# Last layer norm of a hybrid encoder layer: one broadcast product in place of two scalings, shared by two engines

## The chip, the core and the metric

The kernel runs on one core of one Trainium2 chip. Its engines are TensorE (PE in the profile; PEld is its weight load), VectorE (DVE), ScalarE (ACT), GpSimd (POOL) and the queue on which it starts nearly all transfers (SP). Each engine works through its own list of instructions in order and waits where a semaphore tells it to. The metric is device time in microseconds (us), the median of several runs.

## The reference, cut to what matters

One layer over 1024 prompt and 32 sample positions (1056 columns when stored transposed), model width 1024, hidden width 4096, all in float32. The change lies in the last third:

```python
x = _layernorm(ALPHA * x + mix, ln1_g, ln1_b)
hid = jax.nn.relu(x @ w_ff1)
ff = (hid * hid) @ w_ff2
x = _layernorm(ALPHA * x + ff, ln2_g, ln2_b)
# _layernorm: (x - mean) * rsqrt(var + eps) * g + b, over the 1024 features
```

## The kernel before, in words

Features lie on the partitions (8 blocks of 128), positions on the free axis. Every float32 matmul is done as three: each operand is split into a high part in a shorter format and the rest (`split`, L104 to L111: ACT copies the high part in L108, DVE or POOL subtracts it in L111), and `three` (L856 to L860) issues high by high, high by low and low by high.

The second matrix product of the MLP is mostly done by a seven-product scheme (Strassen-Winograd) over halves of the features and of the 1056 columns. Its two blocks of sums, `z`, are four tiles of two feature blocks each. The hidden blocks outside that scheme (`CLASSIC`, four of them) are multiplied plainly, in quarters of 264 columns.

The program from there on is a list of steps. Each step has loads, preparations (`prep`: splits of weights and activations), matmuls and a `post` part. `run` (L1146) writes the loads of a step six steps ahead of its matmuls and its preparations three steps ahead, so this list sets the order on all engines; nothing is reordered afterwards. At the very beginning `run` holds the preparations back to two until the first steps are written.

The end of the list, in order of the matmuls:

- `P4`: four steps of 24 matmuls, the last product that runs over all four feature blocks at once. Its post adds what was kept in buffers (`fold`, L1018, eight on DVE and four on POOL) and then the accumulators (`add_z`, L1011).
- `qs[0]`, `qs[1]` (q0 and q1 below): eight steps each, one for each feature block, of 12 matmuls with the plain weights `ew`. Each ends with an add of the accumulator into `z` on DVE (L1259).
- `M5`: four steps of 24 matmuls (add in L1125). `M3[0]`: four steps of 12 matmuls (add in L1130; M30 below). Each step of M3 needs all four pairs of blocks, that is four weights and four activations, which its preparation `prep3` makes in three groups: pair 0, pair 1, and pairs 2 and 3 together. For each pair DVE first forms the weight by a subtraction (`add_w`, L853), ACT and POOL split it, and ACT and DVE split the activation.
- `qs[2]` (q2), `M3[1]` (M31), `qs[3]` (q3): 8, 4 and 8 steps of 12 matmuls.

An accumulator is one of four slots of PSUM in rotation.

As soon as a quarter of 264 columns is complete in `z`, its layer norm is worked off between the steps that follow. `ln2_parts` (L1218) gives the parts: three totals on POOL (L1225); `centre`, in which PE sums over the partitions (`small_sum`, L1205 to L1208, two matmuls by a matrix of 1/1024), DVE subtracts the mean from the four tiles (L1233), ACT squares (L1235, L1238) and POOL adds the squares (L1239); `root`, another sum on PE, a square root on ACT (L1244) and a reciprocal on DVE (L1245); and `scaled_out` twice, which for each feature block multiplies by gain and reciprocal root on DVE (L1214), adds the bias on ACT (L1215) and starts the store (L1216). A table at the end of the function says behind which step each part stands.

The last quarter, q3, has a form of its own, `last_quarter` (L1262). Behind q3's third step it sums two blocks on PE for an offset (`offset`; L1289 on ACT), which DVE subtracts from blocks 0 to 3 and POOL from blocks 4 to 7 (L1276); it adds blocks and squares as they come (`square`: ACT L1281, DVE L1283 and L1284); and when the last block is there, `end` sums on PE, subtracts the remaining mean (L1311, tiles 0 and 1 on DVE, 2 and 3 on POOL), takes the root (ACT L1314, DVE L1316) and calls `scaled_out` for all eight blocks. q2's last parts stand between q3's steps.

Of the kernel before, what the change touches and what calls it, by code (L numbers as in the profile page):

```python
# [69 lines left out]
def hybrid_layer(ctx, tc, xT, win, wkw, wo, w1, w2, ckT, cv, ckiT, scT, cw, lnp, rb, cst, oh,  # L70
# [621 lines left out]
    st = {}  # L692
# [328 lines left out]
    def ff2_chunk(ci, pairs):  # L1021
# [45 lines left out]

        def by_features(form, xn, place, post, groups):

            got = {p: {} for p in pairs}  # L1070

            def load(p):
                def f():
                    got[p]["raw"] = hidden_raw()
                    nc.sync.dma_start(got[p]["raw"], hd[p, FORM[xn]])
                return f

            def prep(*ps):
                def f():
                    raw = [form(p) for p in ps]  # L1080
                    for p, r in zip(ps, raw):
                        w, x = place(pairs.index(p))
                        split(got[p]["raw"], *x, lo_eng=V)
                        split(r, *w)
                        got[p]["w"], got[p]["x"] = w, x
                return f

            def step(d, cs):
                acc = []

                def mm():
                    acc.append(new_acc())
# [7 lines left out]
            return [load(p) for p in pairs], [prep(*ps) for ps in groups], step  # L1100

# [36 lines left out]
        if ends:  # L1138
            P5 = by_features(lambda p: n1[p], "t1", place5, post5, [(p,) for p in pairs])
            P3 = by_features(lambda p: add_w(A["12", p], n2[p], OP.subtract), "22", place3, post3, [pairs[:1], pairs[1:2], pairs[2:]])  # L1140
            return P1, P2, P6, P7, P4, P5, P3
# [4 lines left out]
    def run(steps, ahead, ahead_load):  # L1146

        n, prepared = len(steps), 0
        for i in range(-ahead_load, n):
            if i + ahead_load < n:  # L1150
                for f in steps[i + ahead_load].load:
                    f()
            while prepared < min(n, i + ahead + 1 if i > 0 else min(2, i + ahead + 1)):
                for f in steps[prepared].prep:
                    f()
                prepared += 1
            if i >= 0:
                for f in steps[i].mm + steps[i].post:
                    f()
# [50 lines left out]

    def scaled_out(c0, n, rstd, js):
        for j in js:
            zj = z[j // 2][:, j % 2, c0:c0 + n]
            V.scalar_tensor_tensor(zj, zj, lnw[:, 2, j:j + 1], rstd, op0=OP.mult, op1=OP.mult)  # L1214
            S.activation(zj, zj, AF.Identity, bias=lnw[:, 3, j:j + 1])  # L1215
            nc.sync.dma_start(yT[j * 128:j * 128 + 128, c0:c0 + n], zj)  # L1216

    def ln2_parts(c0, n):  # L1218
        cols = slice(c0, c0 + n)
# [21 lines left out]
        def root():  # L1241
# [4 lines left out]

        return (total(1), total(2), total(3), centre, root, lambda: scaled_out(c0, n, got["rstd"], range(4)),
                lambda: scaled_out(c0, n, got["rstd"], range(4, 8)))

# [15 lines left out]
    def last_quarter():  # L1265
# [26 lines left out]

        def begin():
            got["sums"] = unit("s1")
            for i in range(4):
                centre(i, V)
                square(i)

        def end():
# [8 lines left out]
            for i in range(4):  # L1308
# [37 lines left out]
    for d in range(3):  # L1346
        P4[1 + d].post.insert(0, fold(d, 0, 1, V))
    (load5, prep5, step5), (load3, prep3, step3) = P5, P3
    M5 = [step5(d, (0, 1)) for d in range(4)]
    M3 = [[step3(d, (c,)) for d in range(4)] for c in range(2)]  # L1350
    steps += qs[0] + qs[1] + M5 + M3[0] + qs[2] + M3[1] + qs[3]
    for j in range(4):
        for m, st in enumerate((qs[0][j // 2], qs[0][4 + j // 2])):
            load, prep = classic_w(j, m)
            st.load.append(load)
            st.prep.append(prep)
        qs[0][5 + j // 2].load.append(load5[j])
        qs[1][3 + j].prep.append(prep5[j])
        M5[1 + j // 2].load.append(load3[j])
    for f, st in zip(prep3, (M5[3], M3[0][0], M3[0][1])):  # L1360
        st.prep.append(f)
    for q, when in ((0, (qs[1][2], qs[1][7], M5[0], M5[1])),
                    (1, (M5[1], M3[0][3], qs[2][2], qs[2][5])),
                    (2, (M3[1][1], qs[3][1], qs[3][2], qs[3][3]))):
        when = (qs[q][3], qs[q][5], qs[q][7]) + when
        for f, st in zip(ln2_parts(q * Q, Q), when):
            st.post.append(f)
# [85 lines left out]
```

## Time and profile before

| what | value |
|---|---|
| device time, median of 3 runs | 1344.34 us (1343.89 to 1350.7) |
| the profiled execution, its own time | 1348.35 us |
| its span (first to last recorded work) | 1346.6 us |
| PE busy | 1245.1 us, 92% of the span |
| DVE busy | 994.9 us, 74% |
| ACT busy | 692.8 us, 51% |
| POOL busy | 564.6 us, 42% |
| granted TensorE clock, mean | 0.967 |

All rows below are of the profiled execution; times are microseconds from the start of its span. The shares are averages over stages with different limits, so what a change in one stage is worth has to be read from that stage's rows.

### The profile page before, as it was taken

Reading aid. Unit: us, or ns where it says so; the run is one execution under the profiler, and the core shown is the slowest. Engines: PE = TensorE matmul, PEld = TensorE weight load, DVE = VectorE, ACT = ScalarE, POOL = GpSimd, SP = SyncE. Lnnn points to the kernel's source line nnn. Section 1 sums busy time; section 2 is a strip of 40 time slices with the busy share of each in tenths; the row PEclk is TensorE's granted clock in tenths of the full one; section 3 lists DMA queues with packets and bytes.
Section 4 is the critical chain, followed back from the end, with each engine's and each line's share of the span. In section 5 each row is a group of like instructions: output and inputs, shape, how many; then the busy total and the mean of one; then the engine's idle time right before and its main releaser. Section 6 shows DMA issues by size and latency. Waiting matters only on the chain. (4 is left out here: it accounts for less than half of the span.)

```text
span 1346.6 us, 24097 instructions
## 1 busy us (share of the span) xinstructions
PE 1245.1 (92%) x8822; PEld 1203.5 (89%) x8822; DVE 994.9 (74%) x2043; ACT 692.8 (51%) x1378; POOL 564.6 (42%) x452
## 2 busy tenths in 40 slices
PE   7999999897899988896899999999999999998984
PEld 6999999897788987785899999999999999998884
DVE  5675899999488889878657667666557668586766
ACT  6666988644688878784322222222343444443323
POOL 2412344513521252363453553454445444447632
PEclk9999999899899998988899999999999999998987
DMA  6221111134531221243134343443863663542201
GB/s 209 92 68 37 48 33 47 48 108 152 166 87 18 47 65 32 71 141 122 45 108 150 138 153 139 147 154 137 302 234 91 196 187 113 176 144 87 65 33 65
DMA packets 97222, 149.98 MB, mean 111 GB/s; under 512 B 12456, under 2 KB 41808, under 8 KB 97104
## 3 DMA queue, kind: packets, MB, share of 16 engines
q1 hardware_dynamic: 81664, 139.55, 31.7%
q0 software_dynamic: 9504, 4.33, 1.9%
q10 hardware_dynamic: 5936, 4.58, 1.2%
q8 instruction: 69, 1.13, 0.4%
q14 instruction: 49, 0.40, 0.1%
HBM read 105.41 MB, written 43.00 MB: 110 GB/s over the span
## 5 line engine op out<-in xcount | busy, mean ns | idle before, releaser
L111 POOL TENSOR_TENSOR whl<-wraw,whl 128x512 fp32r<-128x512 f32 (+1 forms) x184 | 251.0, 1369 | 429.6 <-ACT whl L108 408.8
L858 PE MATMUL acc<-b,whl 128*128 128x264 f32 x1088 | 310.9, 286 | 6.1 <-DVE ring L937 3.0
L859 PE MATMUL acc<-b,whl 128*128 128x264 f32 x1088 | 310.7, 286 | 0.0
L860 PE MATMUL acc<-b,whl 128*128 128x264 f32 x1088 | 309.4, 284 | 0.0
L858 PEld LDWEIGHTS acc<-b,whl 128*128 128x128 f32 x1088 | 205.6, 189 | 7.1 <-DVE ring L937 3.2
L860 PEld LDWEIGHTS acc<-b,whl 128*128 128x128 f32 x1088 | 206.1, 189 | 0.0
L859 PEld LDWEIGHTS acc<-b,whl 128*128 128x128 f32 x1088 | 205.1, 189 | 0.1
L108 ACT ACTIVATE whl<-wraw 128x512 fp32r<-128x512 f32 (+1 forms) x184 | 113.1, 623 | 175.3 <-DVE wraw L853 143.2
L131 PE MATMUL mm<-xh,whl 128*128 128x384 f32 (+4 forms) x520 | 172.3, 332 | 14.3 <-ACT whl L108 5.6
L132 PE MATMUL mm<-area,whl 128*128 128x384 f32 (+4 forms) x552 | 182.9, 332 | 0.4 <-DVE area L111 0.4
L133 PE MATMUL mm<-xh,whl 128*128 128x384 f32 (+4 forms) x520 | 169.6, 331 | 0.0
L111 DVE TENSOR_TENSOR b<-xraw,b 128x528 fp32r<-128x528 f32 x94 | 69.7, 742 | 87.1 <-ACT b L108 87.0
L108 ACT ACTIVATE b<-xraw 128x528 fp32r<-128x528 f32 x94 | 60.5, 644 | 136.0 <-PE acc L860 82.1
L441 ACT ACTIVATE junka<-s,cand 128x1024 bf16<-128x1024 f32 (+1 forms) x93 | 96.5, 1037 | 42.0 <-DVE cand L454 34.2
L131 PEld LDWEIGHTS mm<-xh,whl 128*128 128x128 f32 (+1 forms) x520 | 97.9, 188 | 18.1 <-issue 8.1
L132 PEld LDWEIGHTS mm<-area,whl 128*128 128x128 f32 (+1 forms) x552 | 104.5, 189 | 2.9 <-DVE area L111 0.8
L133 PEld LDWEIGHTS mm<-xh,whl 128*128 128x128 f32 (+1 forms) x520 | 97.6, 188 | 3.2 <-POOL whl L111 1.2
L111 POOL TENSOR_TENSOR whl<-at,whl 128x512 fp32r<-128x512 f32 x56 | 81.5, 1465 | 30.8 <-ACT whl L108 30.8
L443 DVE TENSOR_SCALAR_CACHE_REDUCE junk<-s,cand 128x384 bf16<-128x384 f32 (+1 forms) x124 | 80.2, 647 | 1.3
L858 PE MATMUL acc<-area,whl 128*128 128x264 f32 x240 | 69.0, 288 | 0.0
L859 PE MATMUL acc<-area,whl 128*128 128x264 f32 x240 | 68.7, 286 | 0.0
L860 PE MATMUL acc<-area,whl 128*128 128x264 f32 x240 | 68.5, 286 | 0.0
(310 smaller groups left out, 3345.9 us busy)
## 6 DMA issues: line engine op xcount, KB each, us to landing
hd<-ring SPq DMA_DIRECT2D x98, 264.0 KB, 2.1
xraw<-hd SPq DMA_DIRECT2D x98, 264.0 KB, 2.7
at<-in_w_dram SPq DMA_DIRECT2D x58, 256.0 KB, 3.7
wraw<-in_win_dram SPq DMA_DIRECT2D x52, 256.0 KB, 2.6
wraw<-in_wo_dram SPq DMA_DIRECT2D x40, 256.0 KB, 2.7
w_a<-in_w_dram SPq DMA_DIRECT2D x23, 256.0 KB, 3.7
w_c<-in_w_dram SPq DMA_DIRECT2D x19, 256.0 KB, 3.4
zz<-zd SPq DMA_DIRECT2D x4, 1056.0 KB, 8.4
```

The costliest lines, as they stand in the source:

```text
L108: S.activation(hi, raw, AF.Copy)
L111: (lo_eng or G).tensor_tensor(lo, raw, f32(hi), op=OP.subtract)
L131: PE.matmul(ps, wh[k], a, start=(k == 0), stop=False)
L132: PE.matmul(ps, wh[k], b, start=False, stop=False)
L133: PE.matmul(ps, wl[k], a, start=False, stop=(k == K - 1))
L441: S.activation(junk(R, N), s, AF.Sign, bias=c, scale=-1.0, accum_out=cnt[:R, i:i + 1])
L443: V.tensor_scalar(junk(R, N), s, c, -float(k), op0=OP.is_ge, op1=OP.add, accum_out=cnt[:R, i:i + 1])
L858: PE.matmul(ps, wh, xhi, start=start, stop=False, skip_group_check=more)
L859: PE.matmul(ps, wh, xlo, start=False, stop=False, skip_group_check=more)
L860: PE.matmul(ps, wl, xhi, start=False, stop=stop, skip_group_check=more)
```

## The change

It does several things to the end of the program and one to its middle.

- `scaled_out` is taken apart. `scaled` multiplies a tile (two feature blocks, 128x528) by the reciprocal root, broadcast over the two blocks, on an engine that is given to it; `out` applies gain and bias in one ACT operation for each block and starts the store. Quarters 0 and 2 are scaled on POOL, quarter 1 on DVE, the last on DVE (tiles 0, 1, 2) and POOL (tile 3).
- The parts of the layer norms stand behind other, mostly later steps. Quarter 1's `centre` moves from M5's second step to M30's second, its `root` from M30's fourth step to q2's sixth. `offset` stands one step earlier (behind q3's second step), the offset's subtraction is divided over two steps, and q2's `root` and its scaling and outputs stand two to four steps later in q3.
- Three of the four weights for `prep3` are formed behind q0's fifth to seventh steps (`make`). The low parts of the activations of pairs 1 and 3 are subtracted on POOL instead of DVE.
- The plain weights `ew` are loaded and split for one step at a time, from P4 on, where they were split two at a time from q0 on.
- `run` no longer holds back the first preparations.

```diff
@@ by_features
+            def make(p):
+                def f():
+                    got[p]["form"] = form(p)
+                return f
...
-                    raw = [form(p) for p in ps]
-                    for p, r in zip(ps, raw):
+                    for p in ps:
+                        if "form" not in got[p]:
+                            make(p)()
+                    for p in ps:
                         w, x = place(pairs.index(p))
-                        split(got[p]["raw"], *x, lo_eng=V)
-                        split(r, *w)
+                        split(got[p]["raw"], *x, lo_eng=lo_eng(pairs.index(p)))
+                        split(got[p]["form"], *w)
@@ run
-            while prepared < min(n, i + ahead + 1 if i > 0 else min(2, i + ahead + 1)):
+            while prepared < min(n, i + ahead + 1):
@@ the layer norm
-    def scaled_out(c0, n, rstd, js):
-        for j in js:
+    def scaled(c0, n, rstd, parts, eng):
+        for i in parts:
+            zi = z[i][:, :, c0:c0 + n]
+            eng.tensor_tensor(zi, zi, rstd[:, None].to_broadcast([128, 2, n]), op=OP.mult)
+
+    def out(c0, n, parts):
+        for j in [2 * i + a for i in parts for a in range(2)]:
             zj = z[j // 2][:, j % 2, c0:c0 + n]
-            V.scalar_tensor_tensor(zj, zj, lnw[:, 2, j:j + 1], rstd, op0=OP.mult, op1=OP.mult)
-            S.activation(zj, zj, AF.Identity, bias=lnw[:, 3, j:j + 1])
+            S.activation(zj, zj, AF.Identity, scale=lnw[:, 2, j:j + 1], bias=lnw[:, 3, j:j + 1])
             nc.sync.dma_start(yT[j * 128:j * 128 + 128, c0:c0 + n], zj)
@@ last_quarter, end
-                if i > 0:
-                    scaled_out(c0, n, rstd, range(2 * i - 2, 2 * i if i < 3 else 8))
+            for i, e in ((0, V), (3, G), (1, V), (2, V)):
+                scaled(c0, n, rstd, (i,), e)
+                out(c0, n, (i,))
...
-        steps[2].post.append(offset)
-        steps[3].post.append(begin)
+        steps[1].post.append(offset)
+        steps[2].post.append(lambda: begin(0, 1))
+        steps[3].post.append(lambda: begin(2, 3))
@@ where the parts stand
+        if j < 3:
+            qs[0][4 + j].post.append(make3[j])
-        for m, st in enumerate((qs[0][j // 2], qs[0][4 + j // 2])):
+        for m, st in enumerate((P4[j], qs[0][j])):
...
-                    (1, (M5[1], M3[0][3], qs[2][2], qs[2][5])),
+                         (1, V, (M3[0][1], qs[2][5], M3[1][0], M3[1][2], M3[1][1], M3[1][2], M3[1][3], qs[3][0])),
```

DVE's list from q0's root to M30, before (`wraw` is a formed weight, `area` an activation for M30, `zz` the four tiles of z, `at` the reciprocal root):

```order
L1245 RECIPROCAL at<-at 128x264
L853 TENSOR_TENSOR wraw_6871<-w_b,at 128x512
L111 TENSOR_TENSOR area<-xraw_6872,area 128x528
...
L1214 SCALAR_TENSOR_TENSOR zz_10814<-zz_10814,lnw,at 128x264 x2
L1214 SCALAR_TENSOR_TENSOR zz_10846<-zz_10846,lnw,at 128x264 x2
L1233 TENSOR_TENSOR zz_10514<-zz_10514,acc 128x2x264
...
L853 TENSOR_TENSOR wraw_6871<-w_b,at 128x512 x2
L111 TENSOR_TENSOR area<-xraw_6872,area 128x528 x2
```

The same stretch of DVE's list now (L1257 is the reciprocal, L1132 the add of M5, L1245 the subtraction of `centre`):

```order
L1257 RECIPROCAL at<-at 128x264
L111 TENSOR_TENSOR area<-xraw_6872,area 128x528
L1132 TENSOR_TENSOR zz_10814<-acc,zz_10814 128x528
...
L853 TENSOR_TENSOR wraw_6871<-w_b,at 128x512
L111 TENSOR_TENSOR area<-xraw_6872,area 128x528
...
L1137 TENSOR_TENSOR zz_10514<-acc,zz_10514 128x264 x2
L1245 TENSOR_TENSOR zz_10514<-zz_10514,acc 128x2x264
```

One formed weight and two activations are left in the stretch; the eight scalings of quarter 0 are gone from it and quarter 1's subtraction stands behind M30's first two adds.

POOL's list at the end of the program, before (L1239 adds squares, L1276 subtracts the offset, L1311 the mean):

```order
L1239 TENSOR_TENSOR w_d<-w_d 128x528
L1276 TENSOR_TENSOR zz_10814<-zz_10814,at 128x264 x2
L1276 TENSOR_TENSOR zz_10846<-zz_10846,at 128x264 x2
L1311 TENSOR_TENSOR zz_10814<-zz_10814,at 128x2x264
L1311 TENSOR_TENSOR zz_10846<-zz_10846,at 128x2x264
```

POOL's list there now (L1288 is the offset, L1222 the broadcast product, L1324 the mean):

```order
L1288 TENSOR_TENSOR zz_10846<-zz_10846,at 128x264 x2
L1222 TENSOR_TENSOR zz_10514<-zz_10514,at 128x2x264
L1222 TENSOR_TENSOR zz_10547<-zz_10547,at 128x2x264
L1222 TENSOR_TENSOR zz_10814<-zz_10814,at 128x2x264
L1222 TENSOR_TENSOR zz_10846<-zz_10846,at 128x2x264
L1324 TENSOR_TENSOR zz_10814<-zz_10814,at 128x2x264
L1324 TENSOR_TENSOR zz_10846<-zz_10846,at 128x2x264
L1222 TENSOR_TENSOR zz_10846<-zz_10846,at 128x2x264
```

Quarter 2's four products have come between the offset and the last mean, and one product of the last quarter stands at the end.

ACT's last rows now (L1293 squares, L1317 to L1327 belong to `end`, L1227 is `out`):

```order
L1227 ACTIVATE zz_10514<-zz_10514,lnw 128x264 x2
L1293 ACTIVATE at<-zz_10846 128x264
L1227 ACTIVATE zz_10547<-zz_10547,lnw 128x264 x2
L1227 ACTIVATE zz_10814<-zz_10814,lnw 128x264 x2
L1293 ACTIVATE w_d<-zz_10846 128x264
...
L1327 ACTIVATE at<-w_d,eps 128x264
L1227 ACTIVATE zz_10514<-zz_10514,lnw 128x264 x2
L1227 ACTIVATE zz_10846<-zz_10846,lnw 128x264 x2
L1227 ACTIVATE zz_10547<-zz_10547,lnw 128x264 x2
L1227 ACTIVATE zz_10814<-zz_10814,lnw 128x264 x2
L1227 ACTIVATE zz_10846<-zz_10846,lnw 128x264 x2
```

Six outputs of quarter 2 stand among the last two squares, and its last two stand behind the eight of quarter 3, where ten outputs now end the list instead of eight.

## Rows read from the trace of the kernel before

**Rows 1.** PE's waits from 600 us on: total us, times, longest us

```profile
PE acc L1208 <- DVE w_d L1283: 6.1, 1, 6.1
...
PE acc L858 <- DVE zz L1011: 5.9, 3, 4.5
PE acc L858 <- ACT w L108: 5.1, 1, 5.1
...
PE acc L858 <- ACT ring L908: 1.6, 2, 0.9
```

**Rows 2.** Busy us (instructions) of PE, PEld, DVE, ACT, POOL; PEclk, DMA share, GB/s

```profile
1240.00:1250.00 10.00, 10.00 (x84) 10.00 (x83) 3.54 (x8) 0.00 (x0) 3.12 (x4) 1.00 0.00 0
1280.00:1290.00 10.00, 7.16 (x27) 6.19 (x28) 7.21 (x9) 1.68 (x3) 5.04 (x4) 0.54 0.00 0
```

**Rows 3.** PE's timeline in M30: start, us, line, out<-in [idle before <-releaser]

```profile
1281.28 0.59 PE L858 MATMUL acc<-area,w 128*128 128x264 f32 x1 [5.10 <-ACT w L108]
```

**Rows 4.** The chain that ended last, PE's sum behind M30: start, us

```profile
1292.57 0.89 PE acc L1208 x4
```

**Rows 5.** DVE's timeline from M5 to M30

```profile
1270.27 0.68 DVE L853 TENSOR_TENSOR wraw<-w_b,at 128x512 f32<-128x512 f32 x1
...
1273.33 1.70 DVE L1214 SCALAR_TENSOR_TENSOR zz<-zz,lnw,at 128x264 f32<-128x264 f32 x4
1274.94 2.54 DVE L1233 TENSOR_TENSOR zz<-zz,acc 128x528 f32<-128x528 f32 x4
1277.40 3.16 DVE L853 TENSOR_TENSOR wraw<-w_b,at 128x512 f32<-128x512 f32 x2
1280.49 3.50 DVE L111 TENSOR_TENSOR area<-xraw,area 128x528 fp32r<-128x528 f32 x2
```

**Rows 6.** ACT's timeline at M5's start and before M30's weights

```profile
1262.89 0.48 ACT L1244 ACTIVATE at<-acc,eps 128x264 f32<-128x264 f32 x1 [3.28 <-PE acc L1208]
...
1280.60 0.63 ACT L108 ACTIVATE w<-wraw 128x512 fp32r<-128x512 f32 x1 [1.08 <-DVE wraw L853]
```

**Rows 7.** POOL's timeline, weight splits for M30

```profile
1266.90 1.76 POOL L111 TENSOR_TENSOR whl<-wraw,whl 128x512 fp32r<-128x512 f32 x1
1272.04 1.29 POOL L111 TENSOR_TENSOR whl<-wraw,whl 128x512 fp32r<-128x512 f32 x1 [3.38 <-ACT whl L108]
...
1281.69 3.43 POOL L111 TENSOR_TENSOR w<-wraw,w 128x512 fp32r<-128x512 f32 x2
```

**Rows 8.** DVE's timeline beside a busy POOL, folds and quarter 0's centring

```profile
1223.55 10.41 DVE L1018 TENSOR_TENSOR zz<-zz,w_b 128x528 f32<-128x528 f32 x6
...
1254.41 2.55 DVE L1233 TENSOR_TENSOR zz<-zz,acc 128x528 f32<-128x528 f32 x4 [0.50 <-PE acc L1208]
```

**Rows 9.** POOL's timeline in the same two stretches

```profile
1223.02 3.50 POOL L111 TENSOR_TENSOR ew<-w_d,ew 128x512 fp32r<-128x512 f32 x2
...
1251.25 4.71 POOL L111 TENSOR_TENSOR whl<-w_d,whl 128x512 fp32r<-128x512 f32 x3
```

**Rows 10.** DVE's timeline in the last quarter and at the end

```profile
1319.02 3.20 DVE L1214 SCALAR_TENSOR_TENSOR zz<-zz,lnw,at 128x264 f32<-128x264 f32 x4
...
1332.85 0.42 DVE L1259 TENSOR_TENSOR zz<-acc,zz 128x264 f32<-128x264 f32 x1
...
1337.00 1.80 DVE L1316 RECIPROCAL at<-at 128x264 f32<-128x264 f32 x1
1338.84 3.32 DVE L1214 SCALAR_TENSOR_TENSOR zz<-zz,lnw,at 128x264 f32<-128x264 f32 x8
```

**Rows 11.** POOL's timeline in the last quarter and at the end

```profile
1319.31 3.53 POOL L1276 TENSOR_TENSOR zz<-zz,at 128x264 f32<-128x264 f32 x4 [4.06 <-ACT at L1289]
1335.36 2.56 POOL L1311 TENSOR_TENSOR zz<-zz,at 128x528 f32<-128x528 f32 x2 [12.52 <-ACT at L1307]
```

**Rows 12.** ACT's timeline: last square, and the last eight outputs

```profile
1333.36 0.42 ACT L1281 ACTIVATE w_d<-zz 128x264 f32<-128x264 f32 x1 [0.90 <-DVE zz L1259]
...
1339.36 3.35 ACT L1215 ACTIVATE zz<-zz,lnw 128x264 f32<-128x264 f32 x8 [2.40 <-DVE zz L1214]
```

More of the change, by code (lines that the diff above doesn't have):

```diff
@@ L1066, in product, with by_features @@
             return out
-        def by_features(form, xn, place, post, groups):
+        def by_features(form, xn, place, post, groups, lo_eng):
             got = {p: {} for p in pairs}
@@ L1099, in step @@
                 return Step(mm=[mm], post=[lambda: post(d, acc[0], cs)])
-            return [load(p) for p in pairs], [prep(*ps) for ps in groups], step
+            return [load(p) for p in pairs], [make(p) for p in pairs], [prep(*ps) for ps in groups], step
         def new_pair():
@@ L1138, in ff2_chunk @@
         if ends:
-            P5 = by_features(lambda p: n1[p], "t1", place5, post5, [(p,) for p in pairs])
-            P3 = by_features(lambda p: add_w(A["12", p], n2[p], OP.subtract), "22", place3, post3, [pairs[:1], pairs[1:2], pairs[2:]])
+            P5 = by_features(lambda p: n1[p], "t1", place5, post5, [(p,) for p in pairs], lambda i: V)
+            P3 = by_features(lambda p: add_w(A["12", p], n2[p], OP.subtract), "22", place3, post3, [pairs[:1], pairs[1:2], pairs[2:]],
+                             lambda i: G if i % 2 else V)
             return P1, P2, P6, P7, P4, P5, P3
@@ L1209, in small_sum, with ln2_parts @@
         return ps
-    def scaled_out(c0, n, rstd, js):
-        for j in js:
+    def scaled(c0, n, rstd, parts, eng):
[4 more added lines that the diff above has]
+        for j in [2 * i + a for i in parts for a in range(2)]:
             zj = z[j // 2][:, j % 2, c0:c0 + n]
-            V.scalar_tensor_tensor(zj, zj, lnw[:, 2, j:j + 1], rstd, op0=OP.mult, op1=OP.mult)
-            S.activation(zj, zj, AF.Identity, bias=lnw[:, 3, j:j + 1])
+            S.activation(zj, zj, AF.Identity, scale=lnw[:, 2, j:j + 1], bias=lnw[:, 3, j:j + 1])
             nc.sync.dma_start(yT[j * 128:j * 128 + 128, c0:c0 + n], zj)
-    def ln2_parts(c0, n):
+    def ln2_parts(c0, n, eng):
         cols = slice(c0, c0 + n)
@@ L1245, in root @@
             V.reciprocal(got["rstd"], got["rstd"])
-        return (total(1), total(2), total(3), centre, root, lambda: scaled_out(c0, n, got["rstd"], range(4)),
-                lambda: scaled_out(c0, n, got["rstd"], range(4, 8)))
+        return [total(1), total(2), total(3), centre, root, lambda: scaled(c0, n, got["rstd"], range(2), eng),
+                lambda: scaled(c0, n, got["rstd"], range(2, 4), eng)] + [lambda i=i: out(c0, n, (i,)) for i in range(4)]
     def plain_step(q, d):
@@ L1291, in offset, with begin @@
                 centre(i, G)
-        def begin():
-            got["sums"] = unit("s1")
-            for i in range(4):
+        def begin(*ds):
+            if ds[0] == 0:
+                got["sums"] = unit("s1")
+            for i in ds:
                 centre(i, V)
@@ L1347, in hybrid_layer @@
         P4[1 + d].post.insert(0, fold(d, 0, 1, V))
-    (load5, prep5, step5), (load3, prep3, step3) = P5, P3
+    (load5, _, prep5, step5), (load3, make3, prep3, step3) = P5, P3
     M5 = [step5(d, (0, 1)) for d in range(4)]
@@ L1361, in hybrid_layer @@
         st.prep.append(f)
-    for q, when in ((0, (qs[1][2], qs[1][7], M5[0], M5[1])),
-                    (1, (M5[1], M3[0][3], qs[2][2], qs[2][5])),
-                    (2, (M3[1][1], qs[3][1], qs[3][2], qs[3][3]))):
+    for q, eng, when in ((0, G, (qs[1][2], qs[1][7], M5[3], M3[0][0], M3[0][0], M3[0][1], M3[0][2], M3[0][3])),
+                         (1, V, (M3[0][1], qs[2][5], M3[1][0], M3[1][2], M3[1][1], M3[1][2], M3[1][3], qs[3][0])),
+                         (2, G, (M3[1][1], qs[3][3], qs[3][4], qs[3][5], qs[3][5], qs[3][6], qs[3][6], qs[3][7]))):
         when = (qs[q][3], qs[q][5], qs[q][7]) + when
-        for f, st in zip(ln2_parts(q * Q, Q), when):
+        for f, st in zip(ln2_parts(q * Q, Q, eng), when):
             st.post.append(f)
```

## The prediction

> **What bounds the kernel now.** I first read the list of PE's waits. From 600 us on three waits of 4.5 to 6.1 us stand out in the part that the change touches [rows 1]: the first plain step of q0 waits for an accumulator that DVE's adds (L1011) free, M30 waits for a weight of pair 2 that ACT splits, and the closing sum of q3 waits for DVE's sums. Then the table by stretches: beside an undisturbed stretch with 84 matmuls in 10 us, that is 0.119 us each, the stretch with M30's wait has 27, at a granted clock of 0.54, near the lower of its two levels (1.2 of 2.4 GHz) [rows 2]. So a wait of PE costs itself and a slow time behind it. The timelines then show who made M30 wait. The wait ends at 1281.28 and is 5.10 long [rows 3]. ACT could split the weight at 1280.60, when DVE had formed it [rows 6]. DVE formed it late (two forms in 3.16 from 1277.40) because four scalings of quarter 0 and the four subtractions of quarter 1's centre stood ahead of it (1.70 and 2.54), and then took 3.50 for two activations while POOL split weights [rows 5, 7]. The chain puts M30's end at 1292.57 [rows 4].
>
> Before the end DVE is the bound. PE waits 6.1 for the closing sum, and DVE's last add ends at 1332.85 + 0.42 = 1333.27 [rows 1, 10], so q3's matmuls are done about 7 us before DVE is. From there a chain of single operations runs to the reciprocal's end at 1338.80 [rows 10], and ACT's eight outputs end at 1342.71 [rows 12]; the span ends at 1346.6.
>
> **DVE and POOL in each other's way.** This price decides the second half of the sum. Six folds with both inputs in SBUF take 10.41 on DVE, 1.74 each, while POOL takes 3.50 for two splits, 1.75 each [rows 8, 9]. The subtraction of the mean has the same size, but its second input is in PSUM; it takes 2.55 for four, 0.64 each, although POOL is in the middle of three splits [rows 8, 9]. So the two engines alternate where DVE reads two tiles from SBUF, and each POOL operation then costs DVE about 1.74 - 0.64 = 1.1 us.
>
> **M30, the gain.** The root of quarter 0 hands over to M5 at 1262.9 [rows 6]. M5's first two steps are 48 matmuls, to 1268.6. DVE's two adds behind them (0.64 each by the four from PSUM in [rows 5]) end at 1269.9. Then comes the one form that is left, 0.68 alone or 1.58 beside POOL [rows 5]: 1270.6 to 1271.5. ACT's split takes 0.63 [rows 6]. POOL then has three operations, two weights and the activation that is moved to it, at 1.29 alone to 1.76 beside DVE [rows 7], so that the last low part is there at 1275.1 to 1277.4. M5's four steps end at 1262.9 + 96 x 0.119 = 1274.3, M30's first step needs that part in its last matmul 1.3 us later, at 1275.6. What remains of the wait is 0 to 1.8 us; I take 0.7, since POOL's first operations fall beside DVE's adds from PSUM.
>
> What goes away: the wait of 5.10 [rows 3], and from 1281.28 to 1292.57 the time over what 42 matmuls (half of M30's first step and three whole ones) take at 0.119, that is 11.3 - 5.0 = 6.3. Together 11.4, less the 0.7 that remains: **-10.7**. Quarter 1's sum moves from before M30 into it, and its root from behind M30 into q2; PE does the same sums of 0.89 [rows 4] by q3. In q2 the root has its squares ready: behind M30's weights POOL has four products (1.28 each, below) and three adds of squares, some 10 us from 1277, and q2's sixth step ends near 1290.
>
> **The offset, one step earlier.** The sum now follows at once on q3's second step, and needs DVE's add of that step (0.42 [rows 10]). Just ahead of it on DVE stand the two products of quarter 1's second half, while POOL adds squares of quarter 2; each can wait one POOL operation, 1.1. PE stands still for 0.5 to 2 us; I take **+0.9**.
>
> **The last quarter on DVE.** From the third step's add to the last add DVE has 22 short operations at 0.42 [rows 10] and a reciprocal of 1.80, 11.0 in all; the eight scalings of before (3.20 for four beside POOL [rows 10, 11], 1.7 for four alone) are gone. But POOL now does four products behind that reciprocal, in the stretch in which DVE adds blocks and squares, all from SBUF: up to 4 x 1.1 = 4.4, or nothing if they miss each other. They start with the reciprocal's end and DVE has two such operations in each of the next three steps, so I take 3.5, and 0.7 for POOL's four offsets, which begin before DVE's (beside DVE they took 3.53 [rows 11]). That is 15.2, in which PE does 60 matmuls and a sum, 8.0. DVE again ends 7.2 behind PE: **0**, with ends of -4 and +1.
>
> **The closing.** ACT has two outputs of two blocks, four operations at 0.42 (3.35 for eight [rows 12]), between the last two squares, 1.7 us in a place where before the last square followed DVE's add by 0.09 [rows 10, 12] and the add came some 1.5 behind the square ahead: **+0.75**. Behind the reciprocal DVE needs 0.7 for a tile instead of 0.42 for a block, which costs ACT's start 0.25. Tile 3 then comes from POOL, which starts at the same moment and may wait for DVE's tile; its product I price by the subtraction of the mean, which is broadcast in the same way, 2.56 for two, 1.28 each [rows 11]. So ACT waits about 0.4 more. And ACT's list ends with ten operations instead of eight, because quarter 2's last tile stands behind the last quarter: 0.84. Together **+1.5**.
>
> Each output now has a gain and a bias that differ by partition. No row shows an operation with both, so it costs between nothing and what the whole operation costs now, 0.42. The nearest rows are the single square without either, 0.42, and the outputs with one, 0.42 each in a row of eight [rows 12]: the first operand shows no price there. I take **0** for the second, and keep +2 (half of the upper end, over the ten) as a rival. The Trainium skill (ScalarE: Activation LUTs, section What ACT_TABLE_LOAD costs) speaks against the change here: each per-partition operand of an activation adds about 93 ns there, so an estimate by that page is +0.9 over the ten. No run here shows it so far.
>
> **The edits with little in them.** POOL's and ACT's splits of `ew` move ahead into P4. DVE's folds beside them were already paired with POOL work (1.74 each), and POOL has work to pair there now too: the wait of 4.5 at q0 stays. POOL may stand idle once while the buffer of the second half of `ew` comes free, which lets a fold through: **-0.5**, from -2.5 (the slow time behind it shrinks too) to +0.5. The forms behind q0's steps fall into DVE's idle time there (3.54 busy of 10 [rows 2]): 0. `run`'s two earlier splits concern the start of the first product, where PE waits only for an accumulator, 0.9 at most [rows 1], and never for a weight: 0. The loads of `ew` go out earlier on SP and take 8 places between activations six steps ahead of use: 0. If that cover were missing, an activation would come a load's issue late, and PE has three steps in hand.
>
> **The sum.** -10.7 + 0.9 + 0 + 0.75 + 1.5 + 0 - 0.5 = -8.05, **-8.0**. The profiled execution took 1348.35, so it would take 1340.3. The median of the runs lies 4.0 under it, at 1344.34; the work taken away is the same in both: **1336.3 us**. Half a percent, about what a measurement of this kernel can tell from no change, is 6.7 us.
>
> **Rivals.**
> First, DVE and POOL miss each other in the last quarter. Then DVE ends 3.4 behind PE instead of 7.2: 1332.5. For it: PE's steps leave DVE's adds from PSUM in between. Against it: the folds and the scalings beside POOL's offsets met every time [rows 8, 11]. Here a rule of the Trainium skill also speaks against the change (Perfetto Trace Analysis, section Optimizing Scalar/DVE Operations): since the two engines share a read port, moving work from one to the other might not help. By that rule quarter 2's products give back on POOL what they save on DVE, as in my sum; the folds agree, 1.74 against 0.64.
>
> Second, POOL takes DVE's place ahead of M30. If its six splits all run at 1.76, and DVE's last form is late, PE waits 3 us or more, and the clock may fall as it did at 0.54: 1.8 to 3 of wait and some 3 of slow matmuls are kept. 1341, no change that can be measured. For it: POOL has seven operations in a row there. Against it: the data of the first three are there before M5's second step ends.
>
> Third, the closing costs more: the second per-partition operand at +0.2 in each of the ten. +2: 1338.3, within half a percent.
>
> Fourth, slower than before: a product on POOL isn't priced like a subtraction. No row has a product there. Eight of them stand on the way, four ahead of quarter 1's squares and four in the last quarter, where each holds DVE up. At 3 us each, DVE's end moves by 7 and the tail by 2, and the gain is used up: 1345. From about 4 us each, quarter 1's root makes PE wait in q2 too, and the time is over 1351. Against it: every POOL operation of that size in the rows takes 1.28 to 1.76, whatever it does.
>
> Fifth, the change doesn't move M30's wait: its first half depends on something that the list doesn't show, such as the buffer of the last weights. 1344.
>
> **Chances.** Forecast 0.47 (1334 to 1338.5; a fifth of it within half a percent), first rival 0.17, second 0.16, third 0.10, fourth 0.06, fifth 0.04. Faster by over 0.5%: 0.8 x 0.47 + 0.17 + a part of the third, **0.60**. Within 0.5%: **0.34**. Slower: **0.06**. The range reaches from the first rival with the lower end of the edits at q0 (-2) to the second with 1.5 more: **1330.5 to 1342.5**.
>
> **What would show it.** Right: no wait of PE for `w` in M30 over 1.8 us and a clock of 1.00 there; M30's end near 1282; the wait at q0 still over 3; DVE's sums in the last quarter beside POOL's products at twice their length; ten outputs at the end. Wrong: a POOL product over 2 us, a clock under 0.9 in M30, or DVE's last add more than 9 us behind PE's last matmul of q3.

## The result, and the profile after

The changed kernel took **1336.2 us** (median of six runs; five lie between 1334.8 and 1340.2, and the sixth, disturbed, took 2001.9 at a mean granted clock of 0.56; its profiled execution took 1335.48). Against six runs of the kernel before, with a median of 1348.28, the ratio is 0.9917, with a 95% interval of 0.9898 to 0.9936; a second set of six gave 0.9933 (0.9916 to 0.9951). So it is faster, by 0.5 to 1%, and the forecast of 1336.3 holds. Part of that agreement is luck: the three runs of before that the forecast started from have a median of 1344.34, while seventeen taken later have 1346.92. The change is worth 9 to 11 us, and the forecast said 8.0; the start too low and the gain too small cancel.

PE's waits from 1180 us on, kernel after (total us, times, longest us):

```profile
PE acc L1216 <- DVE w_d L1295: 6.3, 1, 6.3
PE acc L858 <- DVE zz L1011: 3.4, 1, 3.4
PE acc L1216 <- DVE zz L1271: 0.8, 1, 0.8
```

Against [rows 1] the wait for a weight (5.1) is gone, the closing wait of q3 stands as it was (6.1 to 6.3), the one at q0 is 1.1 shorter, and a small one is new: the offset sum that now follows on q3's second step.

The stretches that answer to [rows 2] (columns as there; M30 now runs in the first of them):

```profile
1270.00:1280.00 10.00, 10.00 (x79) 9.69 (x78) 5.94 (x11) 5.15 (x10) 9.92 (x8) 1.00 0.16 54
1280.00:1290.00 10.00, 10.00 (x82) 9.87 (x81) 3.85 (x6) 1.92 (x4) 4.18 (x4) 1.00 0.16 56
```

PE is busy throughout at the full clock, with 79 and 82 matmuls where there were 27 at 0.54. In the first stretch POOL is busy nearly throughout too (9.92 of 10).

DVE's timeline, which answers to [rows 5] (start, us, line, out<-in [idle before <-releaser]):

```profile
1266.46 1.28 DVE L853 TENSOR_TENSOR wraw<-w_b,at 128x512 f32<-128x512 f32 x1
1267.67 0.69 DVE L111 TENSOR_TENSOR area<-xraw,area 128x528 fp32r<-128x528 f32 x1
1268.29 1.31 DVE L1132 TENSOR_TENSOR zz<-acc,zz 128x528 f32<-128x528 f32 x2
...
1275.15 2.55 DVE L1245 TENSOR_TENSOR zz<-zz,acc 128x528 f32<-128x528 f32 x4 [0.46 <-PE acc L1216]
```

POOL's, which answers to [rows 7]:

```profile
1269.74 1.33 POOL L111 TENSOR_TENSOR area<-xraw,area 128x528 fp32r<-128x528 f32 x1
1271.02 1.30 POOL L111 TENSOR_TENSOR w<-wraw,w 128x512 fp32r<-128x512 f32 x1
1272.27 5.21 POOL L1222 TENSOR_TENSOR zz<-zz,at 128x528 f32<-128x528 f32 x4
```

And PE in the last matmuls of M30's first step:

```profile
1272.12 0.28 PE L859 MATMUL acc<-area,w 128*128 128x264 f32 x1
1272.38 0.39 PE L860 MATMUL acc<-area,w 128*128 128x264 f32 x1
```

The one form that is left and the activation take DVE 2 us between M5's adds. POOL's last low part of a weight ends at 1272.32. The matmul that needs it starts at 1272.38, 0.26 behind its neighbour where 0.12 is usual: it came 0.14 too late, and nothing is in hand. A product on POOL takes 5.21 / 4 = 1.30, what the row of the subtraction gave [rows 11].

**One ruler for all runs.** Far ahead of the change two executions of nearly the same kernel differ by several us: a wait of PE for an add of DVE (L1011), 1.0 long in all of them, ends between 1109.2 and 1116.0. The experiments are therefore read from marks near the end: M5's start (ACT's square root of quarter 0), PE's last matmul of q3 (the start of the closing sum less the wait ahead of it), the end of DVE's last add, the end of the last reciprocal, the end of SP's last issue, the end of the span. The columns of the table are the times from one mark to the next; "DVE's lag" is the time by which DVE's last add ends behind PE's last matmul of q3, and "closing" the time from there to the last reciprocal's end.

| kernel | wait at q0 | M5 to q3's end | DVE's lag | closing | to last issue | to the end | sum from M5 |
|---|---|---|---|---|---|---|---|
| before | 4.48 | 63.20 | 7.18 | 5.53 | 4.88 | 2.92 | 83.71 |
| before, second profile | 4.46 | 63.08 | 7.18 | 5.91 | 4.89 | 2.90 | 83.96 |
| after | 3.39 | 52.49 | 7.13 | 5.93 | 6.39 | 2.40 | 74.34 |
| after, second profile | 3.39 | 52.49 | 7.15 | 5.93 | 6.38 | 2.47 | 74.42 |
| forecast of the difference | -0.5 | -9.8 | 0 | +0.75 | +1.5 | not named | -7.55 |

The first row's closing sum and SP's last issues in the kernel before (with [rows 10] and [rows 12] these give its row of the table):

```profile
1332.19 1.25 PE L1208 MATMUL acc<-w_d,cs 128*128 128x264 f32 x2 [6.10 <-DVE w_d L1283]
...
1334.36 1.58 PE L1208 MATMUL acc<-w_d,cs 128*128 128x264 f32 x4
```

```profile
1339.90 3.78 SPq L1216 DMA_DIRECT2D out_dram<-zz  x8
```

The same two places in the kernel after:

```profile
1318.18 1.25 PE L1216 MATMUL acc<-w_d,cs 128*128 128x264 f32 x2 [6.33 <-DVE w_d L1295]
1319.22 1.08 PE L1216 MATMUL acc<-zz,cs 128*128 128x264 f32 x2
1320.10 1.96 PE L1216 MATMUL acc<-w_d,cs 128*128 128x264 f32 x4
```

```profile
1326.33 4.97 SPq L1228 DMA_DIRECT2D out_dram<-zz  x10
```

So the gain is 10.7 between M5 and q3's end and 1.1 at q0; 1.5 is lost in the list of outputs. Another 0.5 is saved behind the last issue; it does not come from the stores (see the account of the forecast).

### The profile page after: what moved, and what is told of

Its sections match the earlier page's. It is cut to its first block, busy times and chain, and to the rows that moved or that the text cites. A ratio compares the mean times of both kernels' runs of the same rounds, so it can differ in the third digit from the quotient of the medians.

```text
span 1333.7 us, 24081 instructions
## 1 busy us (share of the span) xinstructions
PE 1238.0 (93%) x8822; PEld 1197.4 (90%) x8822; DVE 982.2 (74%) x2016; ACT 694.5 (52%) x1378; POOL 578.5 (43%) x463
```

## Experiments on M30

**All of it undone.** Every edit that takes work off DVE ahead of M30 is taken back; the edits of the last quarter stay.

```diff
-            qs[0][4 + j].post.append(make3[j])
-    lambda i: G if i % 2 else V)
+    lambda i: V)
-    (0, G, (qs[1][2], qs[1][7], M5[3], M3[0][0], M3[0][0], ...
+    (0, V, (qs[1][2], qs[1][7], M5[0], M5[1], M5[0], ...
-    (1, V, (M3[0][1], qs[2][5], ...
+    (1, V, (M5[1], M3[0][3], ...
```

> All edits that take work off DVE ahead of M30 undone together: quarter 0's products on DVE behind M5's first two steps, quarter 1's centre behind M5's second step with its root where it stood, the three forms back in the preparation of the weights, all low parts of activations on DVE. The edits of the last quarter stay. Theory (M30's wait and the slow stretch behind it were 10.7 to 11.5 us, and DVE's queue made them): a wait of about 5 for w in M30, a granted clock near 0.54 behind it, and 52.4 to 53.2 us from the root of quarter 0 (M5's start) to the offset sum, where the changed kernel has 41.7; in time about the kernel before, 1346 to 1348. The runs with one edit undone gave 4.0 and 5.8 of it, 9.8 together. Rival (part of the gain comes from elsewhere, such as POOL's better row of splits or PE's earlier arrival): 50 us or less from M5's start to the offset sum, and a time under 1343.

Measured: 1347.67 us, 0.9997 of before (0.998 to 1.0013). From M5's start to q3's end 63.99, to the offset sum 53.2 as the theory had it, and the waits in M30 are back:

```profile
1281.95 0.59 PE L858 MATMUL acc<-area,w 128*128 128x264 f32 x1 [5.05 <-ACT w L108]
1285.36 0.59 PE L860 MATMUL acc<-area,w 128*128 128x264 f32 x1 [2.27 <-POOL w L111]
1286.59 0.59 PE L860 MATMUL acc<-area,w 128*128 128x264 f32 x1 [0.20 <-POOL w L111]
```

with the clock behind them (PE alone: us, busy (instructions), PEclk, DMA share, GB/s):

```profile
1280.00:1285.00 5.00, 1.14 (x2) 0.68 0.00 0
1285.00:1290.00 5.00, 4.44 (x18) 0.50 0.00 0
```

7.5 us of waits and a clock of 0.50 behind them, the lower of its two levels (1.2 of 2.4 GHz), make 63.99 - 52.49 = 11.5. With these edits undone the changed kernel is not measurably faster than before, although all else of the change is in it, the 1.1 at q0 too. The rival, a gain between M5 and the offset sum from elsewhere, falls.

**One edit undone at a time.** First the forms back in the preparation of the weights (the first line of the diff above alone):

> The changed kernel with one part undone: the three weights for M30 are formed in their preparations again, not behind q0's steps. Theory (what took M30's wait away is that DVE's list between M5 and M30 became short, and each part of that counts by its own length): the two last forms then stand behind M5's second step, the last low part comes 2 to 3 us later, and PE waits 1.5 to 3 us in M30; M30 to the end moves by as much, the rest stays. Rival A (the early forms are what took the wait away): 5 us or more of wait comes back, and the granted clock falls to about half behind it. Rival B (they do nothing, the moved centre and outputs did it all): no wait over 0.5 us.

Measured: 1344.77 us in one run. The waits come to 1.8, as expected, but to q3's end it takes 56.49, 4.0 more than with the edit and not only as much as the waits. The waits in M30:

```profile
1277.49 0.39 PE L860 MATMUL acc<-area,w 128*128 128x264 f32 x1 [0.21 <-POOL w L111]
1278.75 0.39 PE L859 MATMUL acc<-area,w 128*128 128x264 f32 x1 [0.76 <-POOL area L111]
1279.98 0.39 PE L860 MATMUL acc<-area,w 128*128 128x264 f32 x1 [0.84 <-POOL w L111]
```

Then quarter 1's centre back behind M5's second step:

```diff
-    (1, V, (M3[0][1], qs[2][5], ...
+    (1, V, (M5[1], M3[0][3], ...
```

> The changed kernel with one part undone: quarter 1's centre stands behind M5's second step again and its root behind M30's fourth. Theory (DVE's list and what is queued on POOL): four subtractions (2.55) and three adds of squares (4.1 on POOL) come ahead of the last two weights, so PE waits 3 to 5 us for a weight in M30, and as long a slow stretch may follow. Rival A (the early forms alone took the wait away): no wait over 1 us.

Measured: 1343.39 us in one run, waits of 1.79, 0.75 and 0.83, and 58.26 to q3's end, 5.8 more. In both kernels the waits are no longer ACT's to end but POOL's, which comes last in the chain of splits, and short ones were followed by a slow stretch. With the forms back, 1.8 us of waits stood ahead of this, at 0.66 with 24 matmuls in 5 us, where 43 run at the full clock:

```profile
1275.00:1280.00 5.00, 3.19 (x23) 1.00 0.00 0
1280.00:1285.00 5.00, 5.00 (x24) 0.66 0.31 108
1285.00:1290.00 5.00, 5.00 (x43) 1.00 0.09 28
```

So each of these two edits is needed: with all of them POOL's last low part comes just in time, and without one PE waits 1.8 or 3.4 us for low parts. 4.0 and 5.8 add up to 9.8 of the 11.5, but they need not add, since each has a slow stretch of its own; what the other edits ahead of M30 give was not measured alone.

**The splits of `ew` back in q0.**

```diff
-        for m, st in enumerate((P4[j], qs[0][j])):
+        for m, st in enumerate((qs[0][j // 2], qs[0][4 + j // 2])):
```

> The loads and splits of ew back where they were (two in each of four steps of q0, none in P4); all else as changed. Theory (the splits of ew in P4 shorten the wait at q0, because POOL stands idle once and lets a fold through): the wait at q0's start is 4.5 again instead of 3.4, and from its end to M5's start 28.2 us pass instead of 27.4; the whole time 1.9 us more than the changed kernel beyond what differs upstream. Rival (the forms behind q0's steps, or chance, made the difference): 3.4 and 27.4.

Measured: 1338.03 us in one run. The wait at q0 is 4.47, and DVE's six folds ahead of it take 10.40 instead of 9.36. That half of the theory holds; in the changed kernel POOL stands still once, and a fold passes it:

```profile
1223.92 1.60 POOL L111 TENSOR_TENSOR ew<-w_d,ew 128x512 fp32r<-128x512 f32 x1 [0.74 <-ACT ew L108]
```

The other half falls: from the wait's end to M5's start it took 27.5, the rival's number. Among all the kernels here with the short wait that time is 27.2 to 28.7, and it goes with the clock behind the wait, not with the edits. PE in the 8 us behind the wait, in the first and in the second profile of the changed kernel:

```profile
1231.94:1239.94 8.00, 8.00 (x53) 0.79 0.00 0
1233.65:1241.65 8.00, 8.00 (x44) 0.64 0.00 0
```

Nine matmuls fewer, at 0.119 each, are 1.1 us, and to M5's start it takes 27.4 in the first and 28.5 in the second. Ordered by this clock, from 0.82 to 0.61, all fourteen profiles stand in the order of that time too, from 27.2 to 28.7. The edit is worth 1.1.

## Experiments on the last quarter

**Quarter 2's products on DVE** instead of POOL:

```diff
-    (2, G, (M3[1][1], qs[3][3], ...
+    (2, V, (M3[1][1], qs[3][3], ...
```

> The changed kernel with quarter 2's four products on DVE instead of POOL. Theory (in the last quarter each POOL product costs DVE 0.9 to 1.1, as much as or more than DVE's own product of 0.66): DVE's last add falls 7.1 us behind PE's last matmul now, and 6 here, since 3.7 of waiting go and 2.6 of work come. Rival (the two engines' work overlaps, and moving the products to POOL relieved DVE): DVE's sums lie 2 us or more later, 9 to 10 us behind PE.

DVE in the changed kernel, beside POOL's four products (1311.38, 5.64 long):

```profile
1311.62 1.35 DVE L1295 TENSOR_TENSOR w_d<-w_d,zz 128x264 f32<-128x264 f32 x1
1312.90 1.52 DVE L1296 TENSOR_TENSOR w_d<-w_d,at 128x264 f32<-128x264 f32 x1
1314.34 0.42 DVE L1271 TENSOR_TENSOR zz<-acc,zz 128x264 f32<-128x264 f32 x1
1314.80 1.07 DVE L1295 TENSOR_TENSOR w_d<-w_d,zz 128x264 f32<-128x264 f32 x1
1315.79 1.52 DVE L1296 TENSOR_TENSOR w_d<-w_d 128x264 f32<-128x264 f32 x1
```

and with the products on DVE:

```profile
1311.67 0.43 DVE L1295 TENSOR_TENSOR w_d<-w_d,zz 128x264 f32<-128x264 f32 x1
1312.18 0.43 DVE L1296 TENSOR_TENSOR w_d<-w_d,at 128x264 f32<-128x264 f32 x1
1312.53 1.32 DVE L1222 TENSOR_TENSOR zz<-zz,at 128x528 f32<-128x528 f32 x2
1313.77 0.43 DVE L1271 TENSOR_TENSOR zz<-acc,zz 128x264 f32<-128x264 f32 x1
```

Four sums from SBUF take 5.46 beside POOL and 1.72 alone, 3.7 more; DVE's own four products take 2.64. So giving them to POOL costs DVE 1.1 more than doing them, and with the products on DVE the lag falls from 7.1 to 6.2 (1334.40 us in one run). The Trainium skill (Perfetto Trace Analysis, section Optimizing Scalar/DVE Operations) says that the two engines share an SBUF read port, so that moving work between them might not help. Here the trace agrees with it. The add from PSUM between the sums keeps its 0.42 beside POOL.

**The gain left out of the outputs** (they carry the bias alone, so what they give lacks the gain's factor):

```diff
-    S.activation(zj, zj, AF.Identity, scale=lnw[:, 2, j:j + 1], bias=lnw[:, 3, j:j + 1])
+    S.activation(zj, zj, AF.Identity, bias=lnw[:, 3, j:j + 1])
```

> The changed kernel with the gain left out of the outputs (each output operation has the bias alone; the result is without the gain). Theory (the second per-partition operand costs about 0.1 in each operation, what the ten last outputs took over the eight of before): the ten outputs at the end take 4.2 us instead of 5.25, and the last square stands 0.4 earlier: the end comes 1.0 to 1.5 earlier against DVE's last add. Rival (the outputs are slower because they wait for DVE's and POOL's products): 5.2 us again.

ACT's outputs without the gain:

```profile
1325.87 0.92 ACT L1227 ACTIVATE zz<-zz,lnw 128x264 f32<-128x264 f32 x2 [2.61 <-DVE zz L1222]
1327.02 3.36 ACT L1227 ACTIVATE zz<-zz,lnw 128x264 f32<-128x264 f32 x8 [0.23 <-POOL zz L1222]
```

and with it, in the changed kernel:

```profile
1325.69 5.25 ACT L1227 ACTIVATE zz<-zz,lnw 128x264 f32<-128x264 f32 x10 [2.61 <-DVE zz L1222]
```

The rival falls. The 5.25 holds a short wait for POOL's tile behind the first two outputs, so the price is better read from four outputs in a row without a wait, of quarter 0, with the gain (first line, the changed kernel) and without it:

```profile
1279.35 2.09 ACT L1227 ACTIVATE zz<-zz,lnw 128x264 f32<-128x264 f32 x4
1279.49 1.73 ACT L1227 ACTIVATE zz<-zz,lnw 128x264 f32<-128x264 f32 x4
```

The second per-partition operand costs 0.36 / 4 = 0.09. The Trainium skill (ScalarE: Activation LUTs, section What ACT_TABLE_LOAD costs) has about 93 ns for each such operand. Here the trace agrees with it. The forecast's nothing was wrong, and the kernel before had shown the price of the first operand: alone, a square took 0.42 [rows 12] and an output with one operand took 0.52:

```profile
1319.53 0.52 ACT L1215 ACTIVATE zz<-zz,lnw 128x264 f32<-128x264 f32 x1 [0.30 <-DVE zz L1214]
```

Yet hardly any of it reaches the end. SP's ten issues take 4.92 without the gain and 4.97 with it, because SP needs 3.78 / 8 = 0.47 for each and becomes the limit as soon as ACT is faster than that. From the last reciprocal to the last issue it is 6.25 against 6.39, so the expected 1.0 to 1.5 did not come.

**All edits of the end undone**: gain and reciprocal again in one DVE operation, offset, quarter 2's parts and their places as before.

```diff
-    steps[1].post.append(offset)
-    steps[2].post.append(lambda: begin(0, 1))
-    steps[3].post.append(lambda: begin(2, 3))
+    steps[2].post.append(offset)
+    steps[3].post.append(lambda: begin(0, 1, 2, 3))
-    (2, G, (M3[1][1], qs[3][3], qs[3][4], qs[3][5], ...
+    (2, V, (M3[1][1], qs[3][1], qs[3][2], qs[3][3])),
```

> The edits at the end undone: quarters 2 and 3 are scaled and given out as before (gain and reciprocal in one DVE operation, the bias alone on ACT), the offset of the last quarter stands one step later again, quarter 2's parts stand where they stood. All edits ahead of q3 stay. Theory (the end edits cost 0.8 at the offset sum, nothing in DVE's lag, 0.4 in the closing, 2.1 in the list of outputs): no wait at the offset sum, lag 7.2, eight outputs in 3.35 at the end; in all 3.3 us faster than the changed kernel, 1333 us. Rival (POOL's products in the last quarter save DVE what they were moved for, and the lag of 7.1 would be above 9 without them, since PE now comes to q3 without a slow stretch): 1336 or slower, with a closing wait over 8.

Measured: 0.9931 of before (0.9914 to 0.9948), beside 0.9933 for the changed kernel, run again for comparison:

> The changed kernel once more, beside the versions below and the kernel before on one chip. Theory: 1336 to 1337 us, 0.991 to 0.992 of before. Its markers should come again: no wait of PE for w in M30, 0.8 at the offset sum, 6.3 at the closing sum, DVE's last add 7.1 behind PE's last matmul of q3, ten outputs in 5.25.

By the marks it is 1.2 better than the changed kernel, not 3.3: 73.18 from M5 to the end. The list of outputs gives its 1.5 back (4.87 to the last issue) and the lag is 7.15, as foretold, so the rival falls: without POOL's products DVE's lag is no longer than with them. But PE loses 0.5 more, since quarter 2's root, earlier again, waits for POOL's squares:

```profile
1301.90 1.16 PE L1216 MATMUL acc<-w_d,cs 128*128 128x264 f32 x4 [1.27 <-POOL w_d L1258]
```

In the kernel before the same root kept PE waiting too, but less:

```profile
1315.30 1.16 PE L1208 MATMUL acc<-w_d,cs 128*128 128x264 f32 x4 [0.54 <-POOL w_d L1239]
```

There POOL's last two adds of squares took 1.33 and 1.31; here they take 1.67 and 1.65, beside two products of quarter 1 that now stand on DVE at that place (2.98 for the two, where two take 1.32 without POOL). The rest of the 3.3 was an error of the expectation, which counted ACT's list (2.1) where SP's issues count (1.5), and 0.4 for a closing that is 0.1 here.

**Outputs in idle time.** Quarter 2's outputs move from between the last squares and from the end of the list into ACT's idle time ahead of and behind the square root. Both kernels leave out the last two of quarter 2's eight output blocks, so they show what the places are worth and are no full versions. In the second kernel quarter 2's products stand on DVE besides.

```diff
             S.activation(mean1, mean, AF.Copy)
+            late_out[0]()
...
                     S.activation(rstd, mean2, AF.Sqrt, bias=eps)
+                    late_out[1]()
+                    late_out[2]()
```

> The changed kernel, but quarter 2's last three tiles are given out by ACT in its idle time of the closing: one ahead of the square root, two behind it, none between the last two squares and none behind the last quarter's own. Theory: the last square follows DVE's last add by 0.1 (1.1 earlier), and the last list has 8 outputs, 4.2, instead of ten in 5.25; together 2.1 us faster than the changed kernel, 1334 us. Rival (the end is set by what follows the outputs, the transfers, and by DVE's and POOL's products, not by ACT's list): within 0.7 us of the changed kernel, with ACT waiting for the products between the outputs.

> As the version with quarter 2's outputs in the gap, and in addition quarter 2's four products on DVE instead of POOL. Theory: 0.9 more, since DVE's own products take 2.6 to 5.3 us where POOL's cost DVE's adds 3.5, and the lag behind PE falls from 7.1 to about 6: 1333 us. Rival (the gain seen with the products on DVE was chance): equal to the version with the outputs in the gap, 1334 us, lag 7 or more.

Measured: 0.992 (0.9902 to 0.9938) and 0.9911 (0.9892 to 0.993) of before. By the marks the first is 0.5 better than the changed kernel, not 2.1, and the second, with a lag of 6.2, 0.9 better than the first, as its theory had it. In the first the last square starts 0.09 behind DVE's last add, 1.0 earlier than in the changed kernel, and the closing is 5.94 all the same. So the last square is not in the way. What sets the closing is PE, which comes out of its wait of 6.3 at half the clock (the columns of the second view: us, PE busy (instructions), PEclk, DMA share, GB/s):

```profile
1316.82 1.25 PE L1216 MATMUL acc<-w_d,cs 128*128 128x264 f32 x2 [6.33 <-DVE w_d L1295]
1317.86 1.09 PE L1216 MATMUL acc<-zz,cs 128*128 128x264 f32 x2
1318.74 1.97 PE L1216 MATMUL acc<-w_d,cs 128*128 128x264 f32 x4
```

```profile
1316.82:1317.82 1.00, 1.00 (x2) 0.50 0.00 0
1317.82:1318.82 1.00, 1.00 (x4) 0.50 0.00 0
1318.82:1319.82 1.00, 1.00 (x4) 0.50 0.03 8
```

Across the profiles the closing moves with PE's last four matmuls: where these take 1.58, 1.67, 1.85 and 1.97, it is 5.53, 5.64, 5.80 and 5.93. The list with eight operations gives 1.0 back (5.39 to the last issue), and 0.45 of that is lost again behind the last issue (2.85).

**Both, with all outputs**, the version that the above points to: quarter 2's products on DVE, two tiles given out between the squares of q3's sixth and seventh step, one ahead of the square root, one behind it.

> All of the computation, with quarter 2's products on DVE and its four tiles given out by ACT in idle time: two between the squares of q3's sixth and seventh step, one ahead of the square root, one behind it. Theory now (SP's issues of the outputs and PE's sums at the lower clock set the end, not the last square): DVE's last add 6.2 behind PE's last matmul of q3 instead of 7.1, the closing unchanged at 5.4 to 5.9, eight outputs in 4.25 and eight issues instead of ten, 1.4 us from M5's start to the end less than the changed kernel, of which 0.5 is given back by the last transfer; 0.1% of the time, which the timing can hardly tell: 1335 us, 0.991 to 0.992 of before. Rival (ACT's outputs between the squares hold up the squares and so DVE's sums): lag 7 or more, no gain.

Measured: 1334.77 us, 0.9912 of before (0.9894 to 0.993). From M5 to the end 72.34, which is 2.0 less than the changed kernel: 0.9 from the lag (6.19), 1.0 from the list (5.38), nothing from the closing (5.95). Beside 0.9917 and 0.9933 for the changed kernel the timing can't tell the two apart; the marks can.

**The kernel before, once more**, for two differences that no edit explained:

> The kernel before, profiled a second time, to see which of its markers come again. Theory (they belong to the kernel): a wait of 4.5 at q0's start, 28.2 us from its end to M5's start, 63.2 from there to PE's last matmul of q3, DVE's last add 7.2 behind that, 5.5 to the end of the last reciprocal, with PE's last four matmuls in 1.58, 4.9 to the end of SP's last issue. Rival for two of them (they are chance of one execution, since the version with ew late had 27.5 and all versions of the changed kernel had 1.67 to 1.97): 27.4 to 27.5 behind q0's wait, 1.9 for the four matmuls and 5.9 for the closing.

The row is in the table. M30 and the lag come again to 0.1. The closing does not: PE's last four matmuls took 1.97 and the closing 5.91, as in the changed kernel. The 5.53 of the first profile was chance: there the granted clock was back at 1.00 from 1335.4 on, before the last of these matmuls, and in the second profile it stayed at 0.50 to their end. Its time behind q0's wait was 27.9, within what the others have.

## Why the forecast was right, point by point

- **M30**, -10.7 forecast with 0.7 of wait left: about -10.9, with 0.1 of wait left. From M5's start to q3's end 10.6 to 10.7 are gone; 0.8 at the offset is new in that stretch, and the 0.5 of quarter 2's root is gone, which the forecast did not name. The mechanism is shown by undoing it, which costs 11.5. The estimate of POOL's row, the last low part 12.2 to 14.5 behind M5's start, was kept at 13.0. The second rival (POOL in DVE's place) was close: POOL's last low part came 0.14 late, and with one edit undone there are waits of 1.8 and 3.4, near the 1.8 to 3 that it named. The fourth (a dear product) failed at 1.30, the fifth (the wait isn't moved) with the wait gone.
- **Offset**, +0.9 forecast, 0.79 measured.
- **The last quarter on DVE**, 0 forecast: the lag is 7.13 against 7.18, and what POOL's products cost DVE's sums, put at 3.5, is 3.7. The first rival, that the two miss each other, falls: four of the six sums met a product.
- **Closing**, +0.75 forecast: 0 (5.93 against 5.91; the 5.53 of the first profile of before was chance). The step that failed is "the last square follows later, so the end does". The square did come 1.0 later, but PE's four sums at half the clock run beside it and end later still. The trace of before had it: two of PE's sums in 1.25 at 1332.19, where four at the full clock take 1.05 to 1.16.
- **Tail**, +1.5 forecast: 1.5 to SP's last issue, by other terms, so its agreement is luck. ACT starts 0.22 later (forecast 0.25). Its list of ten takes 5.25 where eight took 3.35, 1.9 more: the forecast had 0.84 for two operations, 0.4 for POOL's tile, which is mostly hidden, and nothing for the second operand, which costs 0.09 in each. And SP, which the forecast did not look at, gives 0.6 back: in the kernel before, its last issue ended 0.97 behind ACT's list (1343.68 against 1342.71), now 0.36 (1331.30 against 1330.94). The third rival's 0.2 for each operand was 0.09, and without it SP's pace would have set the end.
- **q0**, -0.5 forecast: -1.1, by the very fold that passes POOL. The term was undersized: one meeting costs 1.1 by [rows 8, 9], so one meeting less had to give 1.1.
- **Not foretold**: from SP's last issue to the end 2.3 to 2.5 in most kernels and 2.9 in both profiles of before (also 2.85 in the two with the outputs in idle time). It is not the number of outputs: eight of them in the old form gave 2.37. Nor is it the stores: in all fourteen profiles the last packet of a store lands 1.03 to 1.04 behind the last issue. The difference lies behind that, in the program's last instructions (1.3 to 1.5, against 1.8 to 1.9); what sets it stays open.
- `run`'s earlier splits, at 0: PE's waits from 600 us to P4 differ from those of before by no more than two profiles of one kernel do. This edit had no run of its own.

By the marks the change is worth 9.4 from M5 on and 1.1 at q0, 10.5, which both ratios hold (11 and 9); the forecast's 8.05 was 2.5 short: 0.9 between M5 and q3's end, 0.4 in the closing, 0.6 at q0 and 0.5 behind the last issue. That the last 0.5 comes from the change is not shown.

## What to carry to other kernels

Ask of a wait of TensorE which of the engines in the chain behind it has the work that could stand elsewhere, and count the slow matmuls behind the wait with it: here they cost from half of the waits (4.0 beside 7.5) to more than them (2.2 beside 1.8). Moving four elementwise products from VectorE to GpSimd lost 1.1 us here, where both read two SBUF operands at the same time; look for a place where the other engine reads PSUM or stands idle. At the end of a kernel look at the whole chain to the last issue, the queue that issues the transfers included, before pricing any single operation in it.

## What the runs showed of the hardware

- Short waits were followed by the lower clock: behind 1.8 us of them in three pieces came 5 us at a mean of 0.66, about 2.2 us lost besides.
- PE came out of every wait of 5.4 to 6.3 us at the closing at a clock of 0.50, and the eight matmuls of the sums then ran mostly at that level; the moment at which the clock rises again differs between executions of one kernel (the last four took 1.58 and 1.97). The same shows behind q0's wait: 53 matmuls in 8 us in one profile of the changed kernel, 44 in the other.
- SP's issue of an output takes 0.47 us, more than ACT's operation with one per-partition operand in a row of eight (3.35, 0.42 each); with two operands ACT's operation takes 0.09 more, and ACT sets the pace.
- Beside GpSimd's work VectorE's sums with both inputs in SBUF took 1.07 to 1.52 instead of 0.43; an add with one input in PSUM kept its 0.42.
